# A hybrid decoder layer: second norm's reciprocal applied in the MLP's activation, output projection in groups of two tiles

## The chip, the cores and the metric

The kernel runs on one core of a Trainium2 chip. The metric is the device time in microseconds (us); less is better. The engines are TensorE (PE, matrix products into PSUM), VectorE (DVE), ScalarE (ACT), GpSimd (POOL) and SyncE (SP), which here only issues transfers. Each works through its own instructions in program order.

## The reference

One layer over 1024 positions and 1024 features, in float32:

```
u   = rms_norm(x, norm1_g);  z = u @ w_in
y   = concat(group_norm(conv(z)), retention(z) * silu(gate))
x   = x + y @ w_out
out = rms_norm(x + relu(rms_norm(x, norm2_g) @ w_up)**2 @ w_down, final_norm_g)
```

Here `rms_norm(x, g) = x * rsqrt(mean(x*x) + eps) * g`, with the mean over the features of one token. w_up is 1024 x 4096 and w_down 4096 x 1024. The change touches the third line and the part of the fourth that ends at w_down.

## The kernel before

Features lie on the 128 partitions and tokens along the free axis, in two halves of 512 columns (`hs[0]`, `hs[1]`); an activation is eight tiles of 128 x 1024. For float32 accuracy every factor is split into a rounded high part and the rest: a weight block becomes `wh` (an ACT cast) and `wl` (a DVE subtraction, `split_piece`, L157), an operand likewise becomes the two halves of a unit `U` (`put_hi` L707, `put_lo` L712). A product is then 4 blocks times 3 matmuls: high by high, low operand, low weight.

Weight blocks come as a stream of transfers (`Stream`, L141). `plan` lists the pieces in the order of their use; each `prepare` (L169) makes the next one and puts it into the list `parts`. Four pieces are in hand, since the buffers `wp` (L97) are four: a new cast waits for the oldest piece's last matmul.

The MLP uses a Strassen-Winograd scheme with seven products where a plain 2 x 2 block product has eight. For the first matmul of the MLP the blocks are two tiles of w_up's columns by two halves of the features, and two halves of the features by two token halves. Its right-hand operands are 11, 21, 22 (blocks of the normalised input) and sums of them: t1 = 12 - 11, t2 = 22 - t1, t3 = 22 - 12, t4 = 21 - t2. Block 11 is features 0 to 511 and tokens 0 to 511; 21 has the other features, 12 the other tokens. The weight sums are made by POOL in place (`Left.split`, L195: three when the second product's piece is split, one more at the fifth's). `Pair` (L991) collects the seven products of one pair of column tiles into four blocks of the hidden layer, on which Relu and a square follow on ACT (`put`). `v_split` (L1032) splits such blocks, or sums made by POOL in `v_next`, into units `V`, the operands of the down products.

After the mixer (the part up to `y`) the order of work is written out by hand; no planner decides it, but for the splits of `y` of the second token half, which a small planner with expected engine times places (`tick` L463, `force` L425).

The stages that matter are:

- The output projection (L924 to L943): for each token half, eight tiles, each of two weight blocks, so that w_out is read twice. `out_tile` (L877) adds the result to `x2` (the residual), squares it for the norm (POOL adds the squares up) and writes `un`, the value times norm2_g. In the second half the first half's reciprocal root is ready: sums over partitions by PE (`token_rnorms` L288), then a spread over partitions by PE (`spread` L308), and DVE multiplies `un` by it (`normed` L874) and makes operands 11 and 21. `new_basis` (L902) subtracts, on POOL, one residual block from others, two operations for each odd tile; the down products add into the residual in that basis.
- The MLP's start (L1060 to L1134): fourteen products of the first two pairs (`early`). In between, the second token half's reciprocal is made and multiplied in, and t1 to t4 and 22 are made.
- Seven cycles (L1197 to L1213): each has 14 down products for one block of the hidden layer, with 14 up products for the next one between them. A down product (`down_product` L1136) fills two PSUM banks; `down_take` (L1147) adds them into the residual with DVE. PSUM has eight banks, four in pool `pm` and four in `pr`; down products use `pr`, up products `pm`.
- The last block of w_down and the final norm (L1220 to the end).

Of the kernel before, what the change touches and what calls it, by code (L numbers as in the profile page):

```python
# [16 lines left out]
P = 128  # L17
# [24 lines left out]
UP_FIRST, UP_ORDER = (5, 6, 7, 4, 3), (1, 2, 5, 6, 3, 7, 4)  # L42
# [28 lines left out]
def hybrid_layer(  # L71
# [107 lines left out]
    blocks += [w_out[i, c] for _ in hs for i in range(KT) for c in range(2)]  # L179
# [7 lines left out]
    class Left:  # L187


        def __init__(self, stream, n_, order=UP_ORDER, late=None):  # L190
            self.stream, self.n, self.late = stream, n_, late
            self.five_first = 5 in order[:2]
            self.raw = None

        def split(self, n, h=0):  # L195
# [10 lines left out]
            if n == (2 if self.five_first else 5):  # L206
                s3 = lambda: pool.tensor_sub(a21, a22, a11)
                if self.late is None:
                    s3()
                else:  # L210
                    self.late.append(s3)
# [11 lines left out]
    plan += [next_piece] * (4 * KT)  # L223
# [64 lines left out]
    def token_rnorms(sums_, r, pool_=pr):  # L288

        n = r.shape[-1]  # L290
        b = bank(pool_)
# [16 lines left out]
    def spread(wide, pool_=pr):  # L308

        b = bank(pool_)[:, : len(wide) * P]  # L310
        for c, d in enumerate(wide):
            nc.tensor.matmul(b[:, c * P : (c + 1) * P], d, ident, start=True, stop=True)
        return b
# [402 lines left out]
    def product(n, bank_, mid=None):  # L716
        name = {1: "11", 2: "21", 3: "22", 4: "t4", 5: "t1", 6: "t2", 7: "t3"}[n]
        b = bank(bank_)
        w = parts.pop(0)
        if mid:  # L720
            mm(w, [b], lambda _, k: U[name][k], True, False, range(2))
            mid()
            mm(w, [b], lambda _, k: U[name][k], False, True, range(2, 4))
        else:
            mm(w, [b], lambda _, k: U[name][k], True, True)
# [114 lines left out]

    x2 = [unit(s="x2") for _ in range(KT)]
    for i in range(KT):
        nc.sync.dma_start(x2[i], xT[i * P : (i + 1) * P, :])
    un = [None] * KT
    mixer.close()
    ct = ctx.enter_context(tc.tile_pool(name="ct", bufs=11))
# [12 lines left out]
    def put_block(name, j, src):  # L859
        put_hi(name, j, src)  # L860
        put_lo(name, j, src)

    r_half, wides = [None, None], [None, None]

    def norm_half(half, sums_):
        r = rtok[:, 4 * half : 4 * half + 4]
        if half == 0:
            pool.tensor_add(sums_[0], sums_[0], sums_[1])
        wides[half] = token_rnorms(sums_[: 1 + half], r)

    def norm_spread(half):
        r_half[half] = spread(wides[half])

    def normed(k, half, eng):  # L874
        eng.tensor_mul(un[k][:, hs[half]], un[k][:, hs[half]], r_half[half])

    def out_tile(i, half, ssq):  # L877
        sl = hs[half]
        b = bank()
        for c in range(2):  # L880
            mm(
                parts.pop(0), [b],
                lambda n, k: (y_h[4 * c + k][:, sl], y_l[4 * c + k][:, sl]),
                c == 0, c == 1,
            )
        if not (half and i == KT - 1):
            prepare(2)
        x = x2[i][:, sl]
        dve.tensor_add(x, x, b)
        if i < KT - 1:  # L890
            square_into(sums_[0], x, i == 0)
        else:
# [500 lines left out]
```

## Time and profile before

| what | value |
|---|---|
| time, median of 3 runs | 1122.54 us (1121.5 to 1123.16) |
| time of the profiled execution | 1124.21 us |
| span of its profile | 1122.4 us |
| PE busy, share of the span | 96% |
| DVE, ACT, POOL busy | 82%, 45%, 55% |
| mean granted PE clock | 0.983 |
| output projection | 368 to 462.5 us |
| first two pairs of the MLP | 462.5 to 527.3 us |
| seven down/up cycles | 527.3 to 1063.4 us |
| last block and final norm | 1063.4 to 1122.4 us |

The span runs from the first instruction to the last; the time has about 2 us more around it. A window row gives its start and end, its length, then for each engine the busy us and the count of instructions, then the granted clock (1.00 is full speed), the mean busy share of the DMA engines and GB/s. A group row ends in busy us, mean ns of one instruction, and the idle time before them with what ended it. A timeline row has start and length in us; in brackets stands the idle time ahead of it and its end's cause. Lines read L65 for most DVE, ACT and POOL work, because a helper issues it; the names of the tiles tell them apart.

### The profile page before, as it was taken

The numbers are of one execution on the slowest core, as the hardware profiler recorded it, in microseconds if no ns is written. First come the engines' busy times: TensorE is split into PE (matmuls) and PEld (weight loads), VectorE is DVE, ScalarE is ACT, GpSimd is POOL, SyncE is SP. The second block draws the span as 40 slices with busy tenths as digits, with TensorE's granted clock in tenths as the row PEclk, the third lists the DMA queues.
The fourth block names the chain that finished last, engine by engine and source line by source line (L and its number), as shares of the span: only waits on it lengthen the run. The fifth ranks groups of instructions, "written<-read, shape, count | busy, mean of one in ns | idle before, by whom it ended". The sixth has DMA issues, their size and how long they took to land.

```text
span 1122.4 us, 13758 instructions
## 1 busy us (share of the span) xinstructions
PE 1072.7 (96%) x4880; PEld 885.7 (79%) x4880; DVE 915.3 (82%) x1119; ACT 507.4 (45%) x906; POOL 615.1 (55%) x412
## 2 busy tenths in 40 slices
PE   7999999998798899879999999999999999999997
PEld 6878888887676688747788888888888888888886
DVE  8786486689999846698998979879879789798835
ACT  8211431456336444437354444444544454445553
POOL 6253233447677233586945638638447376385443
PEclk9999999998999999879999999999999999999999
DMA  7311112130121652102021120220211212200204
GB/s 263 141 56 47 29 38 85 38 141 19 38 56 39 225 188 76 38 10 66 29 85 38 57 85 20 66 76 29 66 57 49 74 34 61 85 20 19 66 10 151
DMA packets 40309, 77.73 MB, mean 69 GB/s; under 512 B 4528, under 2 KB 6576, under 8 KB 40240
## 3 DMA queue, kind: packets, MB, share of 16 engines
q1 hardware_dynamic: 40240, 76.85, 21.9%
q8 instruction: 38, 0.62, 0.2%
q14 instruction: 31, 0.25, 0.1%
HBM read 72.64 MB, written 4.19 MB: 68 GB/s over the span
## 4 chain that ended last, share of the span: by engine, by line
PE 79%; DVE 16%; issue 2%; ACT 1%; POOL 1%; DMA 0%; DVEq 0%; POOLq 0%; SPq 0%; ACTq 0%
PE b L365 48%; PE b L1144 22%; PE b L327 4%; DVE wl L65 3%; DVE U L65 2%; DVE r L65 2%; DVE z L65 1%; DVE xs L65 1%; DVE un L65 1%; DVE x L65 1%; DVE cv L65 1%; PE b L294 1%; PE b L574 1%; PE b L542 1%; PE b L576 1%
## 5 line engine op out<-in xcount | busy, mean ns | idle before, releaser
L65 ACT CAST wh<-r 128x512 fp32r<-128x512 f32 x302 | 186.0, 620 | 325.2 <-PE b L365 195.1
L365 PE MATMUL b<-U,wh 128*128 128x512 f32 x992 | 313.6, 396 | 12.5 <-DVE U L65 8.1
L65 DVE TENSOR_TENSOR wl<-r,wh 128x512 fp32r<-128x512 f32 x273 | 251.6, 925 | 60.6 <-ACT wh L65 60.1
L1144 PE MATMUL b<-V,wh 128*128 128x512 f32 x784 | 242.0, 389 | 1.3 <-DVE V L65 1.3
L365 PEld LDWEIGHTS b<-U,wh 128*128 128x128 f32 x992 | 188.2, 190 | 58.7 <-DVE U L65 14.4
L65 POOL TENSOR_TENSOR r<-r,r 128x512 f32<-128x512 f32 x136 | 211.6, 1561 | 40.6 <-DVE wl L65 20.5
L65 DVE TENSOR_TENSOR x<-x,b 128x512 f32<-128x512 f32 (+1 forms) x320 | 200.6, 664 | 21.9 <-PE b L365 12.0
L365 PE MATMUL b<-U,wl 128*128 128x512 f32 x496 | 195.3, 394 | 0.0
L1144 PEld LDWEIGHTS b<-V,wh 128*128 128x128 f32 x784 | 147.1, 188 | 32.7 <-DVE V L65 2.2
L65 POOL TENSOR_TENSOR t<-t,t 128x512 f32<-128x512 f32 x69 | 105.3, 1529 | 108.8 <-ACT t L65 62.0
L1144 PE MATMUL b<-V,wl 128*128 128x512 f32 x392 | 152.8, 390 | 0.4 <-DVE wl L65 0.4
L65 POOL TENSOR_TENSOR V<-t,V 128x512 fp32r<-128x512 f32 x35 | 53.0, 1515 | 124.3 <-ACT V L65 123.9
L365 PE MATMUL b<-uh,wh 128*128 128x512 f32 x320 | 107.2, 400 | 6.1 <-DVE z L65 6.1
L65 ACT ACTIVATE t<-t 128x512 f32<-128x512 f32 x128 | 80.8, 632 | 64.6 <-DVE t L65 62.1
L365 PEld LDWEIGHTS b<-U,wl 128*128 128x128 f32 x496 | 94.4, 190 | 19.2
L365 PE MATMUL b<-uh,wl 128*128 128x512 f32 x320 | 105.8, 396 | 1.9 <-DVE wl L65 1.9
L365 PE MATMUL b<-ul,wh 128*128 128x512 f32 x320 | 105.6, 395 | 0.0
L65 DVE TENSOR_TENSOR t<-t,b 128x512 f32<-128x512 f32 x112 | 76.3, 682 | 32.8 <-PE b L365 30.7
L65 POOL TENSOR_TENSOR wl<-r,wh 128x512 fp32r<-128x512 f32 x29 | 39.4, 1357 | 97.3 <-ACT wh L65 92.0
L1144 PEld LDWEIGHTS b<-V,wl 128*128 128x128 f32 x392 | 73.6, 188 | 16.3 <-DVE wl L65 1.2
L65 DVE TENSOR_TENSOR V<-t,V 128x512 fp32r<-128x512 f32 x63 | 77.0, 1222 | 1.2 <-ACT V L65 1.2
L365 PEld LDWEIGHTS b<-uh,wh 128*128 128x128 f32 x320 | 60.2, 192 | 19.7 <-issue 6.1
(157 smaller groups left out, 1505.9 us busy)
## 6 DMA issues: line engine op xcount, KB each, us to landing
r<-w_up_t SPq DMA_DIRECT2D x64, 256.0 KB, 2.6
r<-w_down_t SPq DMA_DIRECT2D x56, 256.0 KB, 2.6
r<-w_in_t SPq DMA_DIRECT2D x48, 256.0 KB, 2.6
r<-w_out_t SPq DMA_DIRECT2D x32, 256.0 KB, 2.6
xt<-xT SPq DMA_DIRECT2D x16, 256.0 KB, 5.4
xs<-xT SPq DMA_DIRECT2D x8, 512.0 KB, 5.8
x<-xT SPq DMA_DIRECT2D x8, 512.0 KB, 7.0
rope<-rope SPq DMA_DIRECT2D x6, 512.0 KB, 6.4
```

The source lines that it names most:

```text
L65: return f(out, *args, **kw)
L294: nc.tensor.matmul(b[:, c : c + 1], q[:, c * P : (c + 1) * P], ones, start=(i == 0), stop=(i == len(sums_) - 1),)
L327: nc.tensor.matmul(vb[i], a[k][:, tsl], b[k // 2][:, vs], start=(k == 0 and a is uh and b is vh), stop=(k == KT - 1 and a is ul),)
L365: nc.tensor.matmul(b, a[:, k, :], rhs(n, k)[r], start=(start and i == 0), stop=(stop and i == len(ops) - 1),)
L542: nc.tensor.matmul(bs[:, j * P : (j + 1) * P], k[j][:, sl], q[j][:, sl], start=True, stop=True)
L574: nc.tensor.matmul(bo[:, js], vj, sc[:, js], start=True, stop=(S is None))
L576: nc.tensor.matmul(bo[:, js], S[:, js], q[j][:, psl], start=False, stop=True)
L1144: nc.tensor.matmul(b, a, r, start=(i == 0), stop=(i == len(ops) - 1))
```

## The change

- **The reciprocal moves.** Relu(r a) = r Relu(a) for r > 0, so the second norm's reciprocal r is not multiplied into the operands any more. The operands are made from `x2` times norm2_g alone, and after each up block `put` runs one DVE operation, max(c, 0) * r, with r in PSUM, in place of ACT's Relu. The square stays on ACT, one slot later (`put_now`). Both halves' sums and spreads are issued during the MLP's start, after products 2 and 4.
- **The projection goes by groups.** Group j has tiles j and 4 + j and both token halves, in eight steps of 12 matmuls; each weight block is fetched and split once. `group_todo` places operands 11, 21, t1 and the sums for t2 and t3 behind fixed steps, in part of the next group. They are scalar_tensor_tensor on DVE; t1 to t4 were POOL and DVE subtractions.
- **The MLP's start** has a table `rest`: what DVE, ACT and POOL do after each of the fourteen products. `new_basis` for all four odd tiles stands at products 11 and 12, and the second `v_split` at 14.
- **PSUM** after the mixer has pools of 3 (up and tile j), 3 (down and tile 4 + j) and 2 banks (the reciprocal, kept to the end).
- **Order.** Up products run 1, 2, 6, 5, 3, 7, 4, also in the last cycle, so that pair 1's last blocks come in another order, and `last_split` moves with them.

```diff
-UP_FIRST, UP_ORDER = (5, 6, 7, 4, 3), (1, 2, 5, 6, 3, 7, 4)
+UP_ORDER, MLP_ORDER = (1, 2, 5, 6, 3, 7, 4), (1, 2, 6, 5, 3, 7, 4)
...
-    pm = ctx.enter_context(tc.tile_pool(name="pm", bufs=4, space=PSUM))
-    pr = ctx.enter_context(tc.tile_pool(name="pr", bufs=4, space=PSUM))
     mixer = ctx.enter_context(ExitStack())
+    pm = mixer.enter_context(tc.tile_pool(name="pm", bufs=4, space=PSUM))
+    pr = mixer.enter_context(tc.tile_pool(name="pr", bufs=4, space=PSUM))
...
-    blocks += [w_out[i, c] for _ in hs for i in range(KT) for c in range(2)]
+    blocks += [w_out[i, c] for j in range(4) for i in (j, 4 + j) for c in range(2)]
...
-    plan += [next_piece] * (4 * KT)
+    plan += [next_piece] * (2 * KT)
...
-    un = [None] * KT
+    un = [None] * 4
     mixer.close()
+    pm = ctx.enter_context(tc.tile_pool(name="pu", bufs=3, space=PSUM))
+    pr = ctx.enter_context(tc.tile_pool(name="pd", bufs=3, space=PSUM))
+    pn = ctx.enter_context(tc.tile_pool(name="pn", bufs=2, space=PSUM))
...
+    lo_, hi_ = hs
+
+    def scaled(k, half):
+        return x2[k][:, hs[half]], sm[:, G2 + k : G2 + k + 1]
+
+    def put_scaled_hi(name, j, k, half):
+        u = unit(F32R, "U")
+        x, g = scaled(k, half)
+        act.activation(u[:, :H], x, AF.Copy, scale=g)
+        U.setdefault(name, [None] * 4)[j] = (u[:, :H], u[:, H:])
+
+    def put_scaled_lo(name, j, k, half):
+        hi, lo = U[name][j]
+        x, g = scaled(k, half)
+        dve.scalar_tensor_tensor(lo, x, g, f32(hi), ALU.mult, ALU.subtract)
+
+    def less(j, half, to):
+
+        x, g = scaled(4 + j, half)
+        dve.scalar_tensor_tensor(to, x, g, to, ALU.mult, ALU.subtract)
+
+    def sum1(j):
+        dve.tensor_sub(un[j][:, lo_], un[j][:, hi_], un[j][:, lo_])
+
+    def sum2(j):
+        less(j, 1, un[j][:, lo_])
+
+    def sum3(j):
+        less(j, 1, un[j][:, hi_])
+
+    def sum4(j):
+        less(j, 0, un[j][:, lo_])
+
+    sums_ = [tmp(), tmp()]
+
+    def out_evac(i, half, b):
+        x, g = scaled(i, half)
         dve.tensor_add(x, x, b)
-        if i < KT - 1:
-            square_into(sums_[0], x, i == 0)
-        else:
-            act.square(sums_[1], x)
-        if un[i] is None:
-            un[i] = unit(s="un")
-        act.activation(un[i][:, sl], x, AF.Copy, scale=sm[:, G2 + i : G2 + i + 1])
-        if half and i == KT - 1:
-            prepare(2)
-        elif half and i % 2:
-            new_basis(i)
+        square_into(sums_[half], x, i == 0)
+        if i < 4:
+            if un[i] is None:
+                un[i] = unit(s="un")
+            act.activation(un[i][:, hs[half]], x, AF.Copy, scale=g)
...
+    lefts = [Left(down, 1) for _ in range(EARLY)]
+    for n in MLP_ORDER:
         plan += [lambda p=p, n=n: lefts[p].split(n) for p in range(EARLY)]
...
+    def group_todo(j):
+
+        t1 = lambda: un[j][:, lo_]
+        return {
+            2: [lambda: put_scaled_hi("11", j, j, 0)],
+            3: [lambda: put_scaled_lo("11", j, j, 0)],
+            4: [lambda: put_scaled_hi("21", j, 4 + j, 0)],
+            5: [lambda: put_scaled_lo("21", j, 4 + j, 0)],
+            8: [lambda: sum1(j), lambda: put_hi("t1", j, t1())],
+            9: [lambda: put_lo("t1", j, t1())],
+            10: [lambda: sum3(j)],
+            11: [lambda: sum2(j)],
+        }
+
+    def group(j):
+        a, b = j, 4 + j
+        ws, banks = {}, {}
+        steps = [(a, 0, 0), (a, 1, 0), (b, 0, 0), (b, 1, 0), (a, 0, 1), (b, 0, 1), (a, 1, 1), (b, 1, 1)]
+        for s, (i, c, half) in enumerate(steps):
+            if half == 0:
+                ws[i, c] = parts.pop(0)
+            elif j == 0:
+                for idx in range(4 * c, 4 * c + 4):
+                    force(("split", idx, 1))
+            if c == 0:
+                banks[i, half] = bank((pm, pr)[i == b])
...
+            slot()
+            if half:
+                prepare()
+            if c:
+                out_evac(i, half, banks[i, half])
+            for t in todo.get(8 * j + s, []):
+                t()
+            if s == 2 and j in (1, 2):
                 down.fetch(4)
...
+    todo = {}
+    for j in range(4):
+        for at, fs in group_todo(j).items():
+            todo.setdefault(8 * j + at, []).extend(fs)
+    for s, j in ((30, 0), (31, 1)):
+        todo.setdefault(s, []).append(lambda j=j: put_hi("t2", j, un[j][:, lo_]))
+    for j in range(4):
+        group(j)
...
-        ups = [(u, n) for u in range(2) for n in UP_ORDER]
-        if b == NBLK - 2:
-            ups[7:] = [(1, n) for n in DOWN_ORDER]
+        ups = [(u, n) for u in range(2) for n in MLP_ORDER]
...
+        def __init__(self, bank_):
+            self.c, self.bank_ = {}, bank_
+
+        def product(self, n):
+            return product(n, self.bank_)
 
         def put(self, name, c):
-            act.activation(c, c, AF.Relu)
-            act.square(c, c)
             self.c[name] = c
-
-        def take(self, n, b, mid=None, defer=False):
-            ready = None
+            r = r_half[int(name[1]) - 1]
+            dve.scalar_tensor_tensor(c, c, 0.0, r, ALU.max, ALU.mult)
+            later.append(lambda: act.square(c, c))
+
+        def take(self, n, b):
             if n == 1:
                 self.acc = tmp()
                 act.copy(self.acc, b)
             if n == 2:
-                ready = "11", add(self.acc, b)
+                self.put("11", add(self.acc, b))
+            if n == 6:
+                dve.tensor_add(self.acc, self.acc, b)
             if n == 5:
-                self.b5 = b
-            if n in (6, 7, 4):
+                self.both = add(self.acc, b)
+            if n == 3:
+                self.put("12", add(self.both, b))
+            if n == 7:
+                dve.tensor_add(self.both, self.both, b)
+                self.put("22", self.both)
                 dve.tensor_add(self.acc, self.acc, b)
-            if n == 6:
-                self.u4 = add(self.acc, self.b5)
-            if n == 7:
-                ready = "22", add(self.acc, self.b5)
-            if n == 3:
-                dve.tensor_add(self.u4, self.u4, b)
-                ready = "12", self.u4
             if n == 4:
-                ready = "21", self.acc
...
+    early = [Pair((pm, pr)[p]) for p in range(EARLY)]
...
+    rest = [
+        todo[32] + lo("t2", dve, 0, 1) + hi("t2", 2),
+        todo[33] + todo[34] + todo[35] + hi("t2", 3) + lo("t2", dve, 2),
+        lo("t2", dve, 3) + call(sum4, 0, 1) + call(hi22, 0, 1),
+        call(sum4, 2, 3) + call(hi22, 2, 3) + call(lo22, 0),
+        call(lo22, 1) + hi("t3", 0, 1),
+        call(lo22, 2, 3) + hi("t3", 2, 3),
+        lo("t3", dve, 0, 1) + hi("t4", 0),
+        lo("t3", dve, 2) + lo("t3", pool, 3) + hi("t4", 1),
+        lo("t4", dve, 0) + hi("t4", 2),
+        lo("t4", dve, 1) + hi("t4", 3) + lo("t4", pool, 2),
+        lo("t4", pool, 3) + call(new_basis, 1, 3),
+        call(new_basis, 5, 7),
+        [lambda: v_split(early, 1, 0)],
+        [lambda: v_split(early, 1, 1)],
+    ]
+    for at, (n, p) in enumerate((n, p) for n in MLP_ORDER for p in range(EARLY)):
+        b = early[p].product(n)
+        if at == 1:
+            wides = [token_rnorms([sums_[h]], rtok[:, 4 * h : 4 * h + 4]) for h in range(2)]
+            up.fetch(4)
+        if at == 3:
+            r_half[:] = [spread(w, pn) for w in wides]
+        prepare()
+        for f in rest[at]:
             f()
+        put_now()
+        if at == 2:
+            b2 = b
+            continue
+        if at == 3:
+            early[0].take(n, b2)
+        early[p].take(n, b)
...
-                    four[1].append(lambda: last_split(1, "22"))
-                    four[3].append(lambda: last_split(1, "21"))
+                    for f, name in ((four[0], "12"), (four[2], "22"), (four[3], "21")):
+                        f.append(lambda name=name: last_split(1, name))
...
-        new = [Pair(), Pair()]
+        new = [Pair(pm), Pair(pm)]
```

More of the change, by code (lines that the diff above doesn't have):

```diff
@@ L187, in hybrid_layer, with __init__ @@
     class Left:
[L190 to L191 removed]
+        def __init__(self, stream, n_, order=UP_ORDER):
+            self.stream, self.n = stream, n_
             self.five_first = 5 in order[:2]
@@ L306, in token_rnorms, with spread @@
         return wide
-    def spread(wide, pool_=pr):
-        b = bank(pool_)[:, : len(wide) * P]
+    def spread(wide, pool_=None):
+        b = bank(pool_ or pr)[:, : len(wide) * P]
         for c, d in enumerate(wide):
@@ L982, in put_now @@
     def put_now():
-        while later:
-            later.pop(0)()
+        fs, later[:] = list(later), []
+        for f in fs:
+            f()
     def add(a, b):
@@ L1204, in hybrid_layer @@
             else:
-                bk = product(y, pm)
+                bk = pairs[x].product(y)
             prepare()
@@ L1212, in hybrid_layer @@
             else:
-                pairs[x].take(y, bk, defer=True)
-    put_now()
-    last_split(1, "12")
+                pairs[x].take(y, bk)
     for q in range(4):
```

167 lines of the change are left out of this document (26 added, 141 removed).

## The prediction

> **What bounds the kernel now.** I read the totals first, then one window per stage, then TensorE's (PE's) waits between 376 and 610 us.
>
> ```profile
> span 1122.4 us, 13758 instructions
> PE 1072.7 (96%) x4880; PEld 885.7 (79%) x4880; DVE 915.3 (82%) x1119; ACT 507.4 (45%) x906; POOL 615.1 (55%) x412
> ```
> ```profile
> 376.80:462.50 85.70, 85.70 (x379) 71.00 (x380) 50.43 (x67) 43.31 (x75) 28.92 (x20) 0.98 0.47 158
> 462.50:527.30 64.80, 52.39 (x193) 38.71 (x192) 56.03 (x58) 30.52 (x56) 47.12 (x31) 0.84 0.11 33
> 527.30:606.40 79.10, 77.33 (x337) 62.75 (x336) 73.26 (x94) 37.28 (x66) 52.81 (x35) 1.00 0.19 54
> 606.40:682.60 76.20, 76.20 (x337) 63.07 (x337) 66.10 (x91) 35.30 (x61) 44.34 (x29) 1.00 0.19 56
> 987.20:1063.40 76.20, 76.20 (x337) 63.07 (x337) 70.84 (x95) 39.38 (x68) 46.71 (x30) 1.00 0.12 35
> ```
> ```profile
> PE b L365 <- DVE U L65: 8.1, 8, 2.2
> PE b L294 <- POOL t L65: 3.6, 1, 3.6
> PE b L365 <- ACT yh L65: 3.2, 1, 3.2
> PE b L1144 <- DVE V L65: 1.3, 2, 1.0
> ```
>
> The windows list PE, weight load, VectorE (DVE), ScalarE (ACT) and GpSimd (POOL) busy time, then the granted clock. Row 1 is the output projection, row 2 the first two column pairs of the MLP (14 products), row 3 the first of seven down/up cycles, row 4 one of the settled cycles, row 5 the last cycle. A settled cycle is 28 products of 12 matmuls: 76.2/336 = 0.227 us each, 2.72 us a product, and PE never stops. The projection runs at that pace too. The MLP's start does not: 14 x 2.72 = 38.1 us of products take 64.8 us, with DVE and POOL busy for 56 and 47 us, PE waiting for operands U, and the clock at 0.84. So about 25 us are lost there and 79.1 - 76.2 = 2.9 us in the first cycle. This is what the change can win.
>
> **Projection.** Its 384 matmuls stay. 16 of 32 transfers of w_out with their casts and subtractions go, all hidden already, since PE is 100% busy in row 1. SP's queue gets shorter by them. Its eight transfers of x stand where they stood, but tile 4 is now wanted in the fourth step, near 384.7 us, and not in the fifth tile:
>
> ```profile
> x<-xT SPq DMA_DIRECT2D x8, 512.0 KB, 7.0
> 374.52 4.17 SPq L843 DMA_DIRECT2D x<-xT  x8
> ```
>
> Half of the issue time and 7.0 us to landing give 383.6: in time, by 1 us. Operands 11, 21 and t1 are now made between its evictions. DVE is asked for about 16 evictions, 16 wl, 20 operand and 6 y operations: 58, between 36 us (0.62 each) and 100 us (1.75), where the stage has 86; the neighbouring rows below put it near the lower end. If that cover went, the excess would reach PE directly. I cost it at nothing. Two normalisation pieces of PE leave the stage:
>
> ```profile
> 422.69 0.79 PE b L294 x8
> 429.08 0.89 PE b L312 x8
> ```
>
> So the projection, ending at 462.5 now, ends at T = 460.7. Its beginning is less sure. PE already did 20 of its matmuls before this wait, which stays:
>
> ```profile
> 376.07 0.49 PE L365 MATMUL b<-yh,wh 128*128 128x512 f32 x1 [3.16 <-ACT yh L65]
> 376.80 0.62 PE L365 MATMUL b<-yl,wh 128*128 128x512 f32 x1 [0.23 <-DVE yl L65]
> 380.20 0.51 PE L365 MATMUL b<-yh,wh 128*128 128x512 f32 x1
> 374.03 0.67 DVE L65 TENSOR_TENSOR z<-z,b 128x512 f32<-128x512 f32 x1
> 388.48 1.75 POOL L65 TENSOR_TENSOR yl<-z,yh 128x512 fp32r<-128x512 f32 x1
> ```
>
> The new PSUM pools replace the mixer's. If they open only after its last eviction (374.7), those 20 matmuls (4.5 us) end at 379.2 and 3.2 us are lost; if by address, none. The second token half of y is now needed in the fifth step, near 385 us, not in the ninth tile; POOL's part was ready at 390.2 and may be 0 to 3.5 us late. DVE can't gain here, so neither end is below nothing. I take 1 us for both: T = 461.7. The same rows price the throttle: eight starts in 3.40 us after that wait, 1.81 at full pace, so 1.6 us follow a long wait.
>
> **The MLP's start.** All 14 products stay (38.1 us), with 0.9 us of sums and 0.9 us of spreading. The 16 multiplications by the reciprocal go; the sums t1 to t4 leave POOL for DVE. DVE's list becomes 36 operations with both inputs in SBUF, 22 that read PSUM, and about 2 us of small ones. Their prices, minimum, median and maximum in ns, and means of two groups:
>
> ```profile
> L65 DVE TENSOR_TENSOR V<-t,V x63: 679/691/1786, 524.2 to 1045.8; 128x512 fp32r<-128x512 f32 x63
> L65 DVE TENSOR_TENSOR x<-x,b x320: 407/675/689, 378.8 to 1112.5; 128x512 f32<-128x512 f32 x152, 128x256 f32<-128x256 f32 x8
> L65 DVE TENSOR_TENSOR un<-un,un 128x512 f32<-128x512 f32 x4 | 7.0, 1762 | 0.0
> L65 POOL TENSOR_TENSOR r<-r,r 128x512 f32<-128x512 f32 x136 | 211.6, 1561 | 40.6 <-DVE wl L65 20.5
> ```
> ```profile
> 632.90 2.47 DVE L65 TENSOR_TENSOR x<-x,b 128x512 f32<-128x512 f32 x4
> ```
>
> An SBUF-only operation has two prices, 0.62 a piece when alone and 1.75 beside a POOL operation; one with a PSUM input stays at 0.62 (2.47/4). POOL takes 1.29 to 1.75, on average 1.56. With a third of the 36 beside POOL, DVE needs 12 x 1.75 + 46 x 0.62 + 2 = 51.5 us, spread over the same span as the chain that follows; t2, 22, t3 and t4 are each asked for a product or more ahead of their use.
>
> **Two POOL queues.** From T on, in order. (1) The sums of squares: PE wants them after two products and half the sums, T + 5.9. POOL's last addition stands behind the weight sums of both pairs, as it does now:
>
> ```profile
> 462.67 4.95 POOL L65 TENSOR_TENSOR r<-r,r 128x512 f32<-128x512 f32 x3
> 467.58 1.27 POOL L65 TENSOR_TENSOR t<-t,t 128x512 f32<-128x512 f32 x1
> ```
>
> Five operations remain at T: 7.8 us, so PE waits 1.9. This takes the place of the 3.6 us wait. Behind it on PE stand products 2 and 3; the tenth product ends at 5.44 + 0.45 + 1.9 + 0.45 + 8 x 2.72 + 0.9 = T + 30.9, the last at T + 41.8. (2) The first down product's fifth matmul, T + 42.7, needs the low part of V for pair 1, which POOL makes. It is issued after the last product; ahead of it POOL has the last low part of t4 (its cast follows the tenth product's weight cast: T + 32.2, done T + 33.7), eight new-basis subtractions, formerly spread over the projection, and three weight sums. 12 x 1.56 = 18.7: T + 52.4, so PE waits 9.7 us. At 1.29 it waits 6.3, at 1.75 12.2. With the throttle, the cycles begin at T + 41.8 + 9.7 + 1.6 = 514.8 in place of 527.3: **-12.5 us**.
>
> One row speaks for a dearer throttle: 484.00:502.00 is worked with no wait over 2.2 us, yet at a low clock.
>
> ```profile
> 484.00:502.00 18.00, 11.41 (x31) 6.45 (x31) 17.92 (x15) 2.94 (x6) 17.38 (x11) 0.75 0.05 15
> ```
>
> The Trainium skill (TensorE: Matmul & The Clock Gate, What's actually happening) states that the half clock comes after an idle window of about 3.4 us; by that the 1.9 us wait costs no clock and the sum stays, and by this row it may cost another 1.6 us. I leave the wait at 1.9.
>
> **The cycles.** Each gets eight scalar_tensor_tensor (maximum, multiply) on DVE and loses eight Relu passes on ACT, which was never the bound (35.3 of 76.2 us). No row shows this operation with 512 columns and a PSUM input. The nearest:
>
> ```profile
> L65 DVE SCALAR_TENSOR_TENSOR h<-b,rtok,dec 128x256 f32<-128x256 f32 x16 | 7.3, 456 | 15.7 <-PE b L542 15.7
> L65 DVE SCALAR_TENSOR_TENSOR z<-z,sm,r 128x512 f32<-128x512 f32 x8 | 9.3, 1162 | 0.1
> ```
>
> Between 0.62 and 1.75 I take 0.66: one input in PSUM, like x<-x,b. Then DVE's 66.1 us become 71.4 of 76.2. The Trainium skill (SBUF — State Buffer, Who interferes with whom) says that DVE with one SBUF input outside the two-port modes does not contend with GpSimd; by that it is 0.66, and were the rule wrong 1.75.
>
> The down products' pool has three banks, not four, and each product takes two. The second bank of a product must now be the first bank of the one before, emptied. The tightest place:
>
> ```profile
> 628.21 0.61 PE L1144 MATMUL b<-V,wh 128*128 128x512 f32 x2
> 630.92 0.62 PE L365 MATMUL b<-U,wh 128*128 128x512 f32 x2
> 635.00 0.62 PE L1144 MATMUL b<-V,wh 128*128 128x512 f32 x2
> ```
>
> The product begun at 628.21 has its first bank emptied by two of the four additions at 632.90, so at 634.14; the bank is wanted at 635.00. Slack 0.86; one scalar_tensor_tensor ahead of it leaves 0.2, and the next products keep some more. Cost 0 to 0.5 us a cycle; I take **+1** for six. The first cycle begins with DVE caught up but POOL late; between 76.2 and 79.1 I take 77.2, **-1.9**. In the last cycle DVE has 4.7 us more (70.8), and pair 1's operand 21 now comes from the last up product: addition, new operation, square, cast, subtraction are 0.62 + 0.66 + 0.63 + 0.62 + 0.68 = 3.2 us, and PE has 2.72 + 18 x 0.227 = 6.8 us of other work; DVE's lag decides: 0 to 3, I take **+1**.
>
> ```profile
> L65 ACT ACTIVATE t<-t 128x512 f32<-128x512 f32 x128 | 80.8, 632 | 64.6 <-DVE t L65 62.1
> L65 ACT CAST wh<-r 128x512 fp32r<-128x512 f32 x302 | 186.0, 620 | 325.2 <-PE b L365 195.1
> ```
>
> **Sum:** -12.5 - 1.9 + 1 + 1 = -12.4. Against the profiled execution's 1124.2 (span 1122.4 and 1.8 around it) 1111.8; it stood 1.7 above the median of the runs, 1122.5, so for a median 1110.
>
> **Rivals.** (1) POOL reaches V in time, because its queue runs ahead of where I place it: without 9.7 + 1.6 it is 1099. For: POOL is idle for most of T + 8 to T + 30. Against: its order is fixed and the t4 part holds the rest back. (2) DVE becomes the bound of the MLP's start. With half of its 36 operations at 1.75 it needs 58.3 us, 6 more than POOL's 52.4: 1116; with three quarters 68.5, 1126. For: in row 2 it is already busy 56 of 65 us. Against: far fewer POOL operations stand beside it until T + 32. (3) Slower: the new operation contends, at 1.75, in the first half of every cycle, where DVE has no room:
>
> ```profile
> 606.40:644.50 38.10, 38.10 (x169) 31.54 (x169) 37.63 (x49) 18.11 (x32) 27.51 (x18) 1.00 0.15 42
> ```
>
> Four come there: 37.6 + 7.0 = 44.6 us in 38.1. Three banks let DVE lag by 2.72 + 1.36 = 4.1 us at most, and the other 2.4 stop PE: 17 us in seven cycles, 1127. It decides from 1.8 us a cycle. At 0.66 the lag is 40.2 - 38.1 = 2.1 us and fits. For: no row shows the operation. Against: x<-x,b never took over 0.69 in those same stretches.
>
> **Numbers.** Forecast 0.48, own range 1106 to 1115; rival 1 0.20; rival 2 0.20 (0.13 faster, 0.05 same, 0.02 slower); rival 3 0.10; 0.02 for something worse. Faster by over 0.2% (about what can be told from no change) 0.81, within it 0.05, slower 0.14. The range 1098 to 1121 holds the forecast, most of rival 1 and the lower half of rival 2.
>
> **What would show it.** Right: a PE wait of 6 to 12 us at the first V, ended by POOL; one of about 2 us at the sums; none over 1 us for U; cycles of 76.2 to 76.7 us with DVE at 71; the new operation near 0.7. Wrong: U waits as before (rival 2), no V wait (rival 1), cycles over 78 us with PE waiting for evictions (rival 3).

## The result and the profile after

The changed kernel takes 1130.99 us (median of 4 runs, 1130.78 to 1133.19) where the kernel before takes 1122.02 on the same chip: a ratio of 1.0086, with a 95% interval from 1.0067 to 1.0105. It is slower, by 0.9%; 1110 was forecast, 1098 to 1121 as the range. The profiled execution took 1133.19 us with a span of 1131.4.

The totals of the kernel after, and its windows: output projection, MLP's start, first cycle, a settled cycle, last cycle.

```profile
span 1131.4 us, 13621 instructions
PE 1074.3 (95%) x4872; PEld 883.4 (78%) x4872; DVE 916.9 (81%) x1168; ACT 456.5 (40%) x817; POOL 570.8 (50%) x396
```
```profile
375.75:464.40 88.65, 88.65 (x385) 73.35 (x386) 41.36 (x61) 35.04 (x59) 23.10 (x17) 0.98 0.29 99
464.40:514.40 50.00, 44.63 (x202) 35.63 (x200) 43.26 (x55) 24.22 (x44) 25.78 (x18) 0.97 0.21 63
514.40:601.38 86.98, 80.06 (x337) 65.33 (x338) 73.21 (x106) 32.08 (x56) 46.94 (x34) 0.94 0.17 49
601.38:679.55 78.17, 77.10 (x338) 62.84 (x337) 69.90 (x100) 30.42 (x52) 42.27 (x30) 1.00 0.19 54
992.23:1072.47 80.24, 77.71 (x338) 62.70 (x337) 75.79 (x104) 34.19 (x60) 46.43 (x33) 1.00 0.13 37
```

The MLP's start went from 64.8 to 50.0 us, as the change intends. Every cycle after it got longer: the first from 79.1 to 87.0, each of the next five from 76.2 to 78.2, the last to 80.2. PE's waits, first from the projection's start to the first cycle, then in cycles 1 to 5 (us in total, times, longest):

```profile
PE b L361 <- DVE z L65: 6.7, 1, 6.7
PE b L1141 <- DVE V L65: 4.0, 1, 4.0
PE b L361 <- DVE U L65: 3.3, 2, 1.9
PE b L1141 <- POOL V L65: 2.9, 1, 2.9
PE b L1141 <- ACT V L65: 1.1, 1, 1.1
PE b L290 <- POOL t L65: 1.0, 1, 1.0
...
PE b L1141 <- DVE x L65: 5.0, 10, 0.7
```

L361 is the old L365 (up products, projection), L1141 the old L1144 (down products; L1139 and L1142 in some of the kernels below). The last row is new: in the settled cycles PE, which never stopped there, now waits for DVE to empty PSUM banks into x. Measured stage by stage against the prediction's sum, in us:

| term | predicted | measured | off by |
|---|---|---|---|
| projection's end (462.5 before) | 461.7 | 464.3 | +2.6 |
| from there to the first down product | 41.8 | 50.1 | +8.3 |
| its waits for V, with the clock | 11.3 | 9.9 | -1.4 |
| rest of the first cycle | 77.2 | 77.1 | -0.1 |
| six cycles against 76.2 each | +1 | +12.1 | +11.1 |
| the last cycle's own | +1 | +2.0 | +1.0 |
| span | -12.4 | +9.0 | +21.4 |

(The rows add to 21.5 by rounding.) About 0.9 us of the first row is no effect of the change: the mixer's last matmul began at 368.70 here, at 367.77 before. The last cycle's excess of 4.1 is divided: 2.0 as in the five ahead of it, 2.1 in two of its later down products, which take 4.3 and 3.2 us.

### The profile page after: what moved, and what is told of

Same layout as the page of the kernel before. It is cut to its first block, busy times and chain, and to the rows that moved or that the text cites. A ratio compares the mean times of both kernels' runs of the same rounds, so it can differ in the third digit from the quotient of the medians.

```text
span 1131.4 us, 13621 instructions
## 1 busy us (share of the span) xinstructions
PE 1074.3 (95%) x4872; PEld 883.4 (78%) x4872; DVE 916.9 (81%) x1168; ACT 456.5 (40%) x817; POOL 570.8 (50%) x396
## 5 line engine op out<-in xcount | busy, mean ns | idle before, releaser
L65 ACT CAST wh<-r 128x512 fp32r<-128x512 f32 x286 | 177.5, 621 | 458.1 <-PE b L361 238.8
L361 PE MATMUL b<-U,wh 128*128 128x512 f32 x992 | 311.2, 395 | 6.9 <-DVE z L65 3.6
L65 DVE TENSOR_TENSOR wl<-r,wh 128x512 fp32r<-128x512 f32 x257 | 233.8, 911 | 102.2 <-ACT wh L65 100.4
L65 POOL TENSOR_TENSOR r<-r,r 128x512 f32<-128x512 f32 x136 | 198.7, 1463 | 155.0 <-DVE wl L65 100.3
L1141 PE MATMUL b<-V,wh 128*128 128x512 f32 x784 | 246.4, 395 | 15.9 <-DVE x L65 7.4
L65 DVE TENSOR_TENSOR x<-x,b 128x512 f32<-128x512 f32 (+1 forms) x320 | 198.0, 664 | 35.8 <-PE b L361 35.8
L361 PEld LDWEIGHTS b<-U,wh 128*128 128x128 f32 x992 | 188.6, 191 | 49.1 <-DVE U L65 4.5
L361 PE MATMUL b<-U,wl 128*128 128x512 f32 x496 | 195.0, 393 | 0.0
L1141 PEld LDWEIGHTS b<-V,wh 128*128 128x128 f32 x784 | 146.6, 189 | 55.4 <-DVE x L65 16.3
L65 POOL TENSOR_TENSOR t<-t,t 128x512 f32<-128x512 f32 x70 | 108.4, 1554 | 103.8 <-ACT t L65 57.9
L1141 PE MATMUL b<-V,wl 128*128 128x512 f32 x392 | 153.6, 392 | 0.0
L361 PE MATMUL b<-uh,wh 128*128 128x512 f32 x320 | 107.1, 400 | 4.4 <-DVE z L65 4.3
L361 PEld LDWEIGHTS b<-U,wl 128*128 128x128 f32 x496 | 94.5, 191 | 20.1 <-DVE wl L65 0.3
L361 PE MATMUL b<-uh,wl 128*128 128x512 f32 x320 | 105.8, 395 | 1.9 <-DVE wl L65 1.9
L361 PE MATMUL b<-ul,wh 128*128 128x512 f32 x320 | 105.8, 395 | 0.7 <-DVE ul L65 0.7
L1141 PEld LDWEIGHTS b<-V,wl 128*128 128x128 f32 x392 | 74.2, 189 | 15.4
L65 POOL TENSOR_TENSOR V<-t,V 128x512 fp32r<-128x512 f32 x35 | 48.0, 1372 | 63.5 <-issue 41.1
L361 PEld LDWEIGHTS b<-uh,wh 128*128 128x128 f32 x320 | 60.2, 192 | 17.5 <-issue 4.5
L361 PEld LDWEIGHTS b<-uh,wl 128*128 128x128 f32 x320 | 60.9, 191 | 15.3 <-DVE wl L65 2.4
L361 PEld LDWEIGHTS b<-ul,wh 128*128 128x128 f32 x320 | 61.0, 191 | 14.6 <-DVE ul L65 1.6
```

Of the source, the lines that this page charges most:

```text
L65: return f(out, *args, **kw)
L361: nc.tensor.matmul(b, a[:, k, :], rhs(n, k)[r], start=(start and i == 0), stop=(stop and i == len(ops) - 1),)
L1141: nc.tensor.matmul(b, a, r, start=(i == 0), stop=(i == len(ops) - 1))
```

## What delays the settled cycles

DVE's and ACT's timelines around the start of cycle 1, after (601.36 us) and before (606.45 us). Columns: start, length, instruction, and in brackets the idle time ahead with what ended it.

```profile
602.03 1.41 DVE L65 TENSOR_TENSOR wl<-r,wh 128x512 fp32r<-128x512 f32 x1 [0.46 <-ACT wh L65]
603.37 0.68 DVE L65 TENSOR_TENSOR t<-t,b 128x512 f32<-128x512 f32 x1
604.08 0.69 DVE L65 SCALAR_TENSOR_TENSOR t<-t,b 128x512 f32<-128x512 f32 x1
604.75 0.69 DVE L65 TENSOR_TENSOR wl<-r,wh 128x512 fp32r<-128x512 f32 x1
605.36 1.78 DVE L65 TENSOR_TENSOR V<-t,V 128x512 fp32r<-128x512 f32 x1
607.07 2.47 DVE L65 TENSOR_TENSOR x<-x,b 128x512 f32<-128x512 f32 x4
...
604.10 0.62 ACT L65 CAST wh<-r 128x512 fp32r<-128x512 f32 x1 [2.10 <-PE b L1141]
```
```profile
606.64 0.69 DVE L65 TENSOR_TENSOR t<-t,b 128x512 f32<-128x512 f32 x1 [0.57 <-PE b L365]
607.25 0.69 DVE L65 TENSOR_TENSOR wl<-r,wh 128x512 fp32r<-128x512 f32 x1
607.85 0.68 DVE L65 TENSOR_TENSOR V<-t,V 128x512 fp32r<-128x512 f32 x1
608.46 2.47 DVE L65 TENSOR_TENSOR x<-x,b 128x512 f32<-128x512 f32 x4
```

Before, DVE empties the product that ended at 606.45 at once, and begins to empty the first down product 2.0 us into the cycle, while it still runs. After, DVE first waits for ACT's weight cast and splits that weight (602.03), so the product that ended at 601.36 is read at 603.37; the same again at 604.10 and 604.75; the down product's banks are emptied from 5.7 us into the cycle, 3.0 after its end. The cast cannot come earlier: it waits for the matmul whose weight buffer it overwrites (2.10 us, ended by PE), and that product has only just ended. Of the 3.7 us by which the first eviction into x comes later, 1.1 are the subtraction for V at 605.36: so late it falls beside POOL's weight sums (603.58 to 609.68) and takes 1.78 us in place of 0.68.

PE pays at three places only, the second banks of the second, third and fourth down products of the cycle. Their first matmuls start at 608.39, 614.88 and 620.90, later than the pace of 0.227 us by 0.23, 0.87 and 0.44, and the start behind each is 0.11 late: 1.9 of the 2.0 us. The waits listed above are only half of it; the rest the profile counts as busy (77.1 us a cycle against 76.2).

This is a matter of how many weight pieces are in hand. The kernel before ran its cycles with three, not with four as stated in the section on it: its MLP's start calls `prepare` for 13 of the 14 products (`None if last_one else prepare`). The change calls it after all 14. With four pieces and four buffers a product's `prepare` takes the buffer that this very product frees, and in the program it stands ahead of that product's evictions, so every eviction comes behind a cast and a subtraction. With three it takes the buffer of the product before and runs meanwhile. DVE's waits for `wh` rose from 17.0 to 39.0 us (all 140 splits of cycles 1 to 5, after, then before):

```profile
L65 DVE TENSOR_TENSOR wl<-r,wh 128x512 fp32r<-128x512 f32 x140 | 123.4, 881 | 40.0 <-ACT wh L65 39.0
```
```profile
L65 DVE TENSOR_TENSOR wl<-r,wh 128x512 fp32r<-128x512 f32 x140 | 122.9, 878 | 17.0 <-ACT wh L65 17.0
```

## The experiments

The theories are marked by letters in the expectations; theory L is the one above, and D stands in the first of them. All ratios are to the kernel before.

**Three pieces in hand again** (the changed kernel, one `prepare` fewer):

```diff
-        prepare()
+        if at != 13:
+            prepare()
```

> The changed kernel, with one prepare left out (after the fourteenth product of the MLP's start), so that three weight pieces are in hand in the cycles and not four. Theory L (late subtraction): with four pieces and four buffers each cast waits for the product that just ended, and DVE's subtraction for it stands ahead of that product's evictions; three banks turn this into 2.0 us a cycle. L expects cycles of 76.2 to 76.5 us, a last cycle of 77 to 78, and 1117 to 1120 us. Theory D (DVE simply has too much work since it got the scalar_tensor_tensor): cycles stay at 78.2, time 1129 to 1131.

1111.77 us, ratio 0.9903 (0.9886 to 0.9919): one call fewer is worth 19 us by the medians and turns the change into a gain; the time is 5 us below L's range. Its first, a settled and the last cycle:

```profile
515.89:598.36 82.47, 78.92 (x336) 64.10 (x337) 75.91 (x106) 31.96 (x55) 52.34 (x35) 0.98 0.17 52
598.36:674.52 76.16, 76.16 (x337) 63.08 (x336) 68.64 (x100) 30.30 (x52) 45.10 (x29) 1.00 0.19 56
979.16:1055.85 76.69, 76.46 (x337) 63.01 (x336) 72.50 (x103) 33.74 (x59) 47.62 (x31) 1.00 0.12 35
```

PE never stops in the settled cycle, with three banks and all eight new operations in it. The gain is 10.0 us in cycles 1 to 5, 3.6 in the last, and 4.6 in the first, whose first product takes 7.7 us in place of 12.6. That the time is now near the forecast of 1110 is luck: the MLP's start still takes 50.0 us for 41.8, and the waits for V cost 5.0 us for 11.3.

**Four pieces, but prepared behind the evictions** (changed kernel, cycles only):

```diff
-            prepare()
...
+            prepare()
```

> The changed kernel, four pieces in hand and three banks as it has them; in the cycles prepare stands behind the evictions of its slot and not ahead of them. Leaving a prepare out also shifted the weight sums on POOL by a slot, and this run keeps that as it was. Theory L (the subtraction stands ahead of the evictions) expects cycles of 76.2 to 76.6 us and 1115 to 1119 us. The rival (the shift of POOL's weight sums against V was what helped) expects cycles of 78 and 1130.

1116.69 us, ratio 0.9953 (0.9934 to 0.9973; one execution of 3799.58 us, unexplained, is left out of it). Settled cycles are 76.16 us, with the same four pieces, buffers and banks. So the order of split and eviction on DVE is what costs, not the number of pieces by itself. The first cycle stays long, at 85.2 against 82.5 with three pieces; there the shift of POOL's weight sums, the rival, isn't excluded.

**Two banks for up products, four for down products** (changed kernel):

```diff
-name="pu", bufs=3
-name="pd", bufs=3
+name="pu", bufs=2
+name="pd", bufs=4
```

> The changed kernel with PSUM pools of 2, 4 and 2 banks after the mixer in place of 3, 3 and 2: four for the down products, two for the up products. L expects cycles of 76.2 us (a product's banks may be emptied 2.72 us later) and 1118 to 1121 us; D expects 78.2 and 1130, since no DVE work goes. A third reading, that two banks are too few for the up products, would give cycles over 78.2 and PE waits ahead of up products.

1121.23 us, ratio 0.9990 (0.9981 to 0.9999). The cycles are 76.80, 0.6 more than L expected, and the time is just above its range. With a fourth bank all the waits for x are gone, and what is left in cycles 1 to 6 is of another kind:

```profile
PE b L1141 <- POOL V L65: 1.9, 6, 0.3
```

One matmul of each cycle waits for POOL's part of V, and with the late start behind it this makes the 0.6 us.

**The kernel before, with four pieces:**

```diff
-            pair.take(n, b, None if last_one else prepare)
+            pair.take(n, b, prepare)
```

> The kernel before, with the one prepare that it leaves out at the end of the MLP's start put back, so that four pieces are in hand in its cycles too; four banks, no scalar_tensor_tensor. L expects later evictions that four banks nearly hide: cycles of 76.2 to 76.8 us in place of 76.16, and 1122 to 1127 us. If four pieces were bad by themselves, cycles are 78 and the time 1133.

1122.51 us, ratio 1.0001 (0.9989 to 1.0012). The order on DVE is the bad one here too, yet the cycles stay at 76.16 us: DVE's first down eviction of cycle 1 (which begins at 604.98) starts 5.7 us into it, as in the changed kernel.

```profile
605.61 1.41 DVE L65 TENSOR_TENSOR wl<-r,wh 128x512 fp32r<-128x512 f32 x1 [0.46 <-ACT wh L65]
...
610.65 1.87 DVE L65 TENSOR_TENSOR x<-x,b 128x512 f32<-128x512 f32 x3
```

Late evictions alone cost the settled cycles nothing with four banks, and three banks alone cost them nothing with prompt ones (the first experiment). It is the two together that cost 2.0 us a cycle.

**Relu back on ACT, without the reciprocal** (changed kernel; this leaves the second norm's reciprocal out of the computation):

```diff
-            r = r_half[int(name[1]) - 1]
-            dve.scalar_tensor_tensor(c, c, 0.0, r, ALU.max, ALU.mult)
-            later.append(lambda: act.square(c, c))
+
+            def finish():
+                act.activation(c, c, AF.Relu)
+                act.square(c, c)
+
+            later.append(finish)
```

> The changed kernel with Relu on ACT in place of DVE's scalar_tensor_tensor; the second norm's reciprocal is left out of the computation. D expects cycles of 76.2 us and 1117 us. L expects that only the 0.7 us of the new operation go from ahead of the evictions: cycles of 76.8 to 77.4, 1122 to 1126 us.

1126.4 us, ratio 1.0031 (1.0016 to 1.0046). Settled cycles are 78.02, only 0.15 less: the new operation isn't what slows them. L expected 0.8 to 1.4 us less and missed. The reason stands in DVE's row at the start of cycle 1: without the operation ahead of it, the second weight split waits 0.71 us for its cast.

```profile
600.28 0.69 DVE L65 TENSOR_TENSOR wl<-r,wh 128x512 fp32r<-128x512 f32 x1 [0.71 <-ACT wh L65]
```

The new operation had run inside that wait. Its price in the cycles of the changed kernel (ns; minimum, median, maximum):

```profile
L65 DVE SCALAR_TENSOR_TENSOR t<-t,b x59: 686/687/690, 514.8 to 1071.1; 128x512 f32<-128x512 f32 x59
```

The MLP's start gets 3 us shorter (46.9), so there the eight operations do weigh; 1.1 us of it comes back in the first cycle (88.2).

## What bounds the MLP's start

The prediction had POOL's queue end the wait for V. These rows of the kernel after are PE's three waits at the first down product, then DVE's and POOL's work ahead of the last:

```profile
514.33 0.50 PE L1141 MATMUL b<-V,wh 128*128 128x512 f32 x1 [1.09 <-ACT V L65]
518.85 0.79 PE L1141 MATMUL b<-V,wh 128*128 128x512 f32 x1 [4.02 <-DVE V L65]
523.39 0.80 PE L1141 MATMUL b<-V,wh 128*128 128x512 f32 x1 [2.90 <-POOL V L65]
...
520.04 0.68 DVE L65 TENSOR_TENSOR wl<-r,wh 128x512 fp32r<-128x512 f32 x1
...
520.85 1.27 POOL L65 TENSOR_TENSOR r<-r,r 128x512 f32<-128x512 f32 x1 [2.60 <-issue]
522.08 1.26 POOL L65 TENSOR_TENSOR V<-t,V 128x512 fp32r<-128x512 f32 x1
```

POOL's last weight sum starts 0.13 us behind DVE's `wl`, and only then POOL splits V. The profile names nothing that ended POOL's idle 2.6 us ("issue"), but the sum overwrites the raw weights that `wl` is made from, so it has to wait for it: DVE is late.

**New-basis subtractions spread over products 5 to 8** (changed kernel):

```diff
-        call(sum4, 2, 3) + call(hi22, 2, 3) + call(lo22, 0),
-        call(lo22, 1) + hi("t3", 0, 1),
+        call(sum4, 2, 3) + call(hi22, 2, 3) + call(lo22, 0) + call(new_basis, 1),
+        call(lo22, 1) + hi("t3", 0, 1) + call(new_basis, 3),
...
-        lo("t3", dve, 0, 1) + hi("t4", 0),
-        lo("t3", dve, 2) + lo("t3", pool, 3) + hi("t4", 1),
+        lo("t3", dve, 0, 1) + hi("t4", 0) + call(new_basis, 5),
+        lo("t3", dve, 2) + lo("t3", pool, 3) + hi("t4", 1) + call(new_basis, 7),
...
-        lo("t4", pool, 3) + call(new_basis, 1, 3),
-        call(new_basis, 5, 7),
+        lo("t4", pool, 3),
+        [],
```

> The changed kernel with the eight new-basis subtractions of POOL after products 4, 5, 7 and 8 of the MLP's start, in place of 11 and 12. The prediction's theory (POOL's queue sets when V is ready) expects the waits at the first down product (8.0 us in three pieces) to fall below 2 us and 1121 to 1123 us. The rival (DVE is the bound of the MLP's start, and its low part of V is as late as POOL's) expects 3 us less at most: 1127 to 1130. If the subtractions beside DVE's operands slow it earlier, the wait for 22 grows from 1.9 us.

1131.51 us, ratio 1.0080 (1.0065 to 1.0095), no different from the change; both forecasts were lower. POOL's queue ahead of V is shorter by eight operations, and the first product still takes 10.7 us against 12.6; what it wins is lost at the ninth product, which takes 9.8 us in place of 6.3: there DVE's operations now run beside POOL's. POOL's queue isn't the bound.

**Both splits of V three to four products earlier** (on top of three pieces):

```diff
-        lo("t3", dve, 2) + lo("t3", pool, 3) + hi("t4", 1),
-        lo("t4", dve, 0) + hi("t4", 2),
+        lo("t3", dve, 2) + lo("t3", pool, 3) + hi("t4", 1) + [lambda: v_split(early, 1, 1)],
+        lo("t4", dve, 0) + hi("t4", 2) + [lambda: v_split(early, 1, 0)],
...
-        [lambda: v_split(early, 1, 0)],
-        [lambda: v_split(early, 1, 1)],
+        [],
+        [],
```

> The changed kernel with three pieces in hand, and the two splits of V for the first down product after products 8 and 9 of the MLP's start in place of 13 and 14. If the waits at that product (5.0 us there in the run with three pieces) come from the place of the splits, 3 to 5 us go: 1107 to 1109 us. If DVE's whole list up to the middle of the first cycle is the bound, the wait comes back at the next products, for banks, and the time stays at 1110 to 1112.

1110.67 us, ratio 0.9906 (0.9888 to 0.9923): no different from three pieces alone by the intervals. The first product falls from 7.7 to 4.7 us, but the next three down products take 5.4, 3.7 and 4.3 us for want of emptied banks; the first cycle grows from 82.5 to 83.5. In that cycle:

```profile
PE b L1142 <- DVE x L65: 4.4, 3, 2.4
```

The waits came back at the next products, as the second forecast had it: DVE's list is late as a whole.

**The mixer's PSUM pools kept** (on top of three pieces: four and four banks, and no new pools):

```diff
-    pm = mixer.enter_context(tc.tile_pool(name="pm", bufs=4, space=PSUM))
-    pr = mixer.enter_context(tc.tile_pool(name="pr", bufs=4, space=PSUM))
+    pm = ctx.enter_context(tc.tile_pool(name="pm", bufs=4, space=PSUM))
+    pr = ctx.enter_context(tc.tile_pool(name="pr", bufs=4, space=PSUM))
...
-    pm = ctx.enter_context(tc.tile_pool(name="pu", bufs=3, space=PSUM))
-    pr = ctx.enter_context(tc.tile_pool(name="pd", bufs=3, space=PSUM))
-    pn = ctx.enter_context(tc.tile_pool(name="pn", bufs=2, space=PSUM))
...
-            r_half[:] = [spread(w, pn) for w in wides]
+            r_half[:] = [spread(w, pm) for w in wides]
```

> The changed kernel with three pieces in hand and the mixer's PSUM pools kept to the end: four banks for down products, four for up products of which the two reciprocals hold two. The projection's first bank then doesn't wait for the mixer's last eviction (6.7 us, of which 20 matmuls ahead of y's last tile hid about 4.5 in the kernel before), so 2 to 3 us go there; the bank waits of the first and the last cycle (about 2 us) go too: 1106 to 1109 us. If two banks are too few for the up products, or POOL's V becomes the next wait, 1110 to 1112.

1108.55 us, ratio 0.9881 (0.9860 to 0.9902). The interval overlaps that of three pieces alone; the profile shows the gain, 92.4 us from the start of the mixer's last matmul to the projection's end, where three pieces alone take 95.6. The projection's first wait is again the one that the kernel before has, and the last cycle is 76.16 too. What the changed kernel showed at that place, and then this one's wait:

```profile
375.75 0.77 PE L361 MATMUL b<-yh,wh 128*128 128x512 f32 x1 [6.66 <-DVE z L65]
...
374.93 0.67 DVE L65 TENSOR_TENSOR z<-z,b 128x512 f32<-128x512 f32 x1
```
```profile
PE b L361 <- ACT yh L65: 3.2, 1, 3.2
```

The new pools opened only after the mixer's last eviction (374.93 + 0.67 = 375.60), and no projection matmul started earlier.

**The same without the new-basis subtractions** (part of the residual's change of basis isn't computed):

```diff
-        lo("t4", pool, 3) + call(new_basis, 1, 3),
-        call(new_basis, 5, 7),
+        lo("t4", pool, 3),
+        [],
```

> The kernel with three pieces in hand and the mixer's PSUM pools kept (1108.55 us), with POOL's eight new-basis subtractions of the MLP's start left out, so part of the residual's change of basis isn't computed. In that kernel POOL works on them from 497.0 to 509.2 us, and DVE's six SBUF-only operations in that stretch take 1.77, 1.70, 1.75, 1.69, 1.11 and 1.60 us in place of 0.68; PE waits 2.8 us for the last part of t4 and 2.3 us for V, and the granted clock is 0.71 behind them. Theory C (sharing with POOL sets DVE's list): these operations fall to 0.7 us, DVE is done about 5 to 6 us earlier, the two waits shrink to 0 to 1 us each and the half clock behind them goes too; cycles begin 4 to 6 us earlier and the first is 77 to 79.5 us; time 1100 to 1104 us. Rival N (the number of operations sets it, whoever stands beside): operations stay above 1.2 us or the waits stay, time 1107 to 1109 us. If only the wait for V goes, which POOL's own V operation could also cause, 1105 to 1107 us.

1103.84 us, ratio 0.9831 (0.9813 to 0.9849). DVE near the same place, with POOL's subtractions beside it (pools kept) and without:

```profile
500.51 1.70 DVE L65 TENSOR_TENSOR wl<-r,wh 128x512 fp32r<-128x512 f32 x1
502.14 1.75 DVE L65 TENSOR_TENSOR U<-un,U 128x512 fp32r<-128x512 f32 x1
503.81 0.68 DVE L65 TENSOR_TENSOR t<-t,b 128x512 f32<-128x512 f32 x1
504.52 0.69 DVE L65 SCALAR_TENSOR_TENSOR t<-t,b 128x512 f32<-128x512 f32 x1
```
```profile
500.64 0.68 DVE L65 TENSOR_TENSOR wl<-r,wh 128x512 fp32r<-128x512 f32 x1
501.25 0.68 DVE L65 TENSOR_TENSOR U<-un,U 128x512 fp32r<-128x512 f32 x1
501.85 0.68 DVE L65 TENSOR_TENSOR t<-t,b 128x512 f32<-128x512 f32 x1
502.56 0.69 DVE L65 SCALAR_TENSOR_TENSOR t<-t,b 128x512 f32<-128x512 f32 x1
```

The two operations with both inputs in SBUF fall from 1.7 to 0.68; the two that read PSUM don't change. The wait for t4 (2.8 us) is gone, and the MLP's start is 4.6 us shorter, 46.6 against 51.2. The wait for V stays, at 2.1 us, and the first cycle is 80.1, longer than C expected, so theory C holds for t4 and not for V: at the last split of V, DVE (1.79 us for that split) shares with POOL's weight sums, which are still there. The Trainium skill (SBUF — State Buffer, Who interferes with whom) states this division: two SBUF inputs contend with a reading GpSimd, at most one, outside the two-port modes, doesn't. These rows agree, 1.7 against 0.68.

**All three mends together** (three pieces, pools kept, V early):

```diff
-        prepare()
+        if at != 13:
+            prepare()
...
+    pm = ctx.enter_context(tc.tile_pool(name="pm", bufs=4, space=PSUM))
+    pr = ctx.enter_context(tc.tile_pool(name="pr", bufs=4, space=PSUM))
...
+        lo("t3", dve, 2) + lo("t3", pool, 3) + hi("t4", 1) + [lambda: v_split(early, 1, 1)],
+        lo("t4", dve, 0) + hi("t4", 2) + [lambda: v_split(early, 1, 0)],
```

> Three pieces in hand, the mixer's PSUM pools kept, and both parts of the second split of V issued three to four products earlier. Without the kept pools the earlier split moved the waits from V to the emptying of banks in the first down products and gained nothing that counts (1110.67 against 1111.77 us). Theory (DVE's list is the bound of the MLP's start, whatever its order): 1106.5 to 1109 us, the first cycle 79.5 to 83 us with its excess spread over the first four down products. Rival (with four banks for the down products the lag is absorbed, so that an early V gains its whole wait): 1103 to 1106 us, first cycle 77 to 79 us. Cycles 1 to 6 are 76.16 by both.

1106.89 us, ratio 0.9867 (0.9852 to 0.9883): it beats both kernels, by 24.1 us the changed one and by 15.3 the one before (1122.2 beside these runs). By the intervals it is no different from the kept pools without an early V. The first cycle is 82.2 us, as the list theory had it, but its fifth product alone takes 6.4, where the theory spread the excess over four; an early V isn't worth its whole wait even with four banks.

## Why the prediction was wrong

- **The step that failed is the one on the cycles:** "Slack 0.86; one scalar_tensor_tensor ahead of it leaves 0.2 ... Cost 0 to 0.5 us a cycle". The slack was read from a trace of the kernel before, in which three pieces are in hand, and carried over to a kernel that keeps four. The 0.66 for the new operation was right (0.687 measured); the weight split that moved ahead of the evictions was not counted. The moved `prepare` was in the diff, as a call without a condition in place of one that leaves out the last product. The place was right: the stops come at the second banks, where the prediction looked for them. The step cost 11.1 of the 21.4 us, and the mend by one call confirms it: settled cycles of 76.16.
- **The signs to look for misled.** "Cycles over 78 us with PE waiting for evictions" was to mean that the new operation contends (rival 3). The sign came, the cause didn't: no instance in the cycles is above 0.69, and without the operation the cycles are 0.15 us shorter. That rival 3's 1127 us comes nearest to the measured 1131 is luck.
- **The MLP's start was mis-sized by 8.3 us.** The price of DVE's list was right: 51.5 us forecast, 50.6 busy (464.27 to 521.87). Its course in time was not: DVE idles 5.3 us for casts and 2.1 for the root early in the stretch, and operations at 1.7 come late, beside POOL. So 22 is late by 1.9 us (4.0 with the slow starts around that wait), t4 by 1.4 (1.7), and ACT's part of V, ahead of the first down product, by 1.1 (1.3). The spreads of both token halves take 1.7 us, where the sum has 0.9, the price of one. Rival 2's figure of 58.3 us for DVE was close by luck (the list ends 57.8 after the projection): it counted slow operations, where 7.4 us of the 57.8 are idle. Its whole, 1116, missed for the cycles.
- **The wait for V was right in size by luck and wrong in cause:** 11.3 us forecast with the clock; 9.9 measured in the first down product and 1.3 ahead of it, ended by ACT, DVE and POOL in turn (1.1, 4.0 and 2.9 us of waiting). "Two POOL queues" took POOL's order for the bound; shortening that queue gained nothing, and POOL was waiting for DVE's `wl`.
- **The half clock.** The prediction weighed a wait of 1.9 us for the sums and left it without a price for the clock; that wait came as 1.0 us and had none. The wait for 22 tells (PE, kernel after):

```profile
495.00 0.80 PE L361 MATMUL b<-U,wh 128*128 128x512 f32 x1 [1.91 <-DVE U L65]
495.59 0.63 PE L361 MATMUL b<-U,wl 128*128 128x512 f32 x1
496.02 1.05 PE L361 MATMUL b<-U,wh 128*128 128x512 f32 x2
...
498.40 0.62 PE L361 MATMUL b<-U,wh 128*128 128x512 f32 x2
```

  Starts are 0.43 us apart until 498.2, then 0.23: eight starts took 3.40 us, 1.6 more than at full pace, the same price that the prediction had read behind a wait of 3.16 us. By the Trainium skill (TensorE: Matmul & The Clock Gate, What's actually happening) an idle window of about 3.4 us has to come first; here it didn't, and the low-clock row that the prediction quoted against that rule was the better guide. But not every short wait has this price: behind the 1.40 us for t4 (508.37) no start is more than 0.34 us after the one before, and in the kernel before the same holds behind a wait of 2.33 us (336.96). What decides between them stays open.
- **The handover** lay within its bounds, 0 to 3.2 us, near the upper one: 6.66 in place of 3.16 us of waiting, and no matmul done ahead of it. From the start of the mixer's last matmul (368.70, before 367.77) to the projection's end it is 95.57 us, where the prediction's 460.7 makes 92.93: 2.6 us. The prediction took 1.
- **Right:** the projection runs at PE's pace with its whole new list of DVE work hidden (5.44 us for each of its later tiles), the sums' wait is 1.0 (1.9 forecast), and the first cycle behind V takes 77.1 (77.2).

## What to carry to other kernels

Count the pieces in hand against the buffers at each change of stage: when they are equal, a preparation waits for the product that has just ended, and whatever stands behind it in the same in-order queue, evictions above all, inherits that wait. Slack that is read from a trace holds only for the order of work in that trace; check that the changed code keeps it, calls without their old conditions included. When PSUM banks are taken away and evictions delayed in one change, test the two apart: each alone cost the settled cycles nothing here.

## What was not expected of the hardware

A wait of only 1.9 us was followed by 3.2 us at half clock, and waits of 1.40 and 2.33 us were not. The new PSUM pools, opened over the old ones' banks, held back every matmul until the old pools' last eviction: 6.66 us of idle PE, against 3.2 with the old pools kept. Dependent DVE operations start 0.71 us apart where independent ones are 0.60 apart (603.37 to 604.08 against 607.25 to 607.85, above; behind such an addition in the kernel after, 512.50 to 513.10).
